# Small loads moved to GpSimd's DMA queue, stores issued later in the program, bias corners filled with the pair's scores

## The chip, the cores and the metric

The kernel runs on one core of a Trainium2 chip. The core has five engines that run side by side and wait for each other through semaphores: TensorE (PE in the profile, with PEld for its weight loads), VectorE (DVE), ScalarE (ACT), GpSimd (POOL) and SyncE (SP). A transfer between the chip's main memory and the on-chip memory is started by an instruction on the queue of one engine; here only SP starts any before the change. Each engine takes its instructions strictly in the order in which the program writes them. The metric is the device time of one execution in microseconds (us); lower is better.

## The reference

One inference step of a two-layer encoder on 320 tokens: 256 frames of a new stream ("prompt") and 64 next frames of an older one ("sample"). Cut to what matters:

```python
for l in range(2):
    h = x @ w_in[l]                                  # 1024 -> 3656 columns
    qa, ka, va, qb, kb, vb, qi, ki, wi = split(h)    # 8 heads of 64 each, twice; 8 index heads
    qb, kb, qi, ki = rope(qb), rope(kb), rope(qi), rope(ki)
    # A: 64-frame chunks read their own and earlier chunks, plus a learned bias of the distance
    oa = softmax(qa @ [cache_a_k, ka] / 8 + rel_bias[clip(distance)]) @ [cache_a_v, va]
    # B: an index score picks k keys for each query, attention over those
    score = sum_h wi[h] * relu(qi[h] @ [cache_b_kidx, ki])
    ob = softmax(over the top k of score)(qb @ [cache_b_k, kb] / 8) @ [cache_b_v, vb]
    x = layer_norm(alpha * x + concat(oa, ob) @ w_out[l])
    x = layer_norm(alpha * x + relu(x @ w_up[l])**2 @ w_down[l])
# returned: x, and ka, va, kb, vb, ki of both layers
```

## The kernel before

Activations are kept transposed (features on the 128 partitions, the 320 tokens along the free dimension), all in 32 bits. Every matrix product is done in three passes (`mm3`, L185 to L191): a weight block is split into a rounded high part `wh` and a rest `wl`, the activation likewise, and TensorE adds high x high, high x low and low x high (L188, L189, L190).

**Weights.** They come in units of 128 output columns (101 units in a layer). `load_raw` (L143) loads two units at a time, 1 MB, into one of two buffers `raw` (L151). `prefetch` (L160) has ScalarE write `wh` (L170), four units ahead of TensorE; a little later `split_rest` (L175) has VectorE write `wl` (L176), and when the second unit of a pair is split the `raw` buffer is free and the next load is written on SP. ScalarE's L170 waits for its load, and everything behind it on ScalarE waits too.

**Order of the work.** There is no scheduler: `manual_schedule` keeps each engine's instructions in the order in which the Python code writes them. A pretended clock (`clock`) moves on by `NEXT` (0.408 pretended us) with every `mm3`. `later(dt, fn)` (L118) puts a step on an agenda, and `advance` (L121) runs steps that are due between two `mm3`. `WAIT` (L46) holds the delays, by layer and by kind of step.

**Attention.** Heads go in pairs; `Pair` (L355) makes the tiles of one pair: queries, keys, values, and for kind A six loads of bias (`bias_tiles`, L333: for each of two heads a 128x128, a 128x256 and a 64x320 piece, L341) and two loads of cached keys and values (L367, L368). In a bias tile two 64x64 corners must hold a very negative number: GpSimd writes them (L342, L343) right behind the load. When a query tile is ready, GpSimd makes its "sample blocks" (`sample_blocks`, L346: one copy L351, two fills L352 and L353); the scores of the sample tokens (TensorE L396, or L535 for the index queries `qi`) wait for them. `scores` (L383), `peaks` (VectorE adds the bias, L410), `exps`, `normalise`, `turn` and `output` follow. The index (`Index`, L475) has four query tiles qi0 to qi3, taken in the order 0, 3, 2, 1; `dots` (L522) multiplies each with the keys (L533, L535).

**Stores.** New keys, values and index keys are stored by SP (L308, L317, L499, L771), written in the program at once behind the step that makes the tile, while that step still has to run on its engine.

All small tiles share 67 buffers named `u`.

Of the kernel before, what the change touches and what calls it, by code (L numbers as in the profile page):

```python
# [16 lines left out]
P = 128  # L17
# [16 lines left out]
NEG = -1.0e30  # L34
# [7 lines left out]
N_SIDE = 4  # L42
N_WARM = 7
N_TAIL = 4
TOKENS = slice(0, P), slice(P, 2 * P), slice(T - P, T)
WAIT = [{"lo": 3.4, "rope": 4.6, "scores": 3.4, "peaks": 0.0, "exps": 1.0, "normalise": 5.6, "turn": 3.0,  # L46
         "output": 2.0, "finish": 4.0, "value": 5.2, "keys": 6.0, "dots": 10.8, "clip": 0.0, "weigh": 0.2,
# [22 lines left out]
def encoder_step(ctx: ExitStack, tc: tile.TileContext, a: dict):  # L70
    nc = tc.nc
# [19 lines left out]
    def main_acc():  # L91
        return acc("mm", 8 - N_SIDE)
# [4 lines left out]
    def side_banks(n, fn, *args):  # L97

        if held[0] + n > N_SIDE:
            later(NEXT, fn, *args)  # L100
            return None
        held[0] += n
        return [acc("at", N_SIDE) for _ in range(n)]

    def release(n):
        held[0] -= n

    def unit(dt=F32, w=T):
        return st([P, 3 * P], "u", N_UNIT, dt)[:, :w]

    def temp(tag, bufs):
        return st([P, T], tag, bufs)
# [5 lines left out]
    def later(dt, fn, *args):  # L118
        agenda.append((clock[0] + dt, len(agenda), fn, args))

    def advance(dt):  # L121
        clock[0] += dt
        while agenda:
            i = min(range(len(agenda)), key=lambda i: agenda[i][0])
            if agenda[i][0] > clock[0]:
                break
            _, _, fn, args = agenda.pop(i)
            fn(*args)

    def flush():  # L130
        while agenda:
            advance(NEXT)
# [48 lines left out]
    def until(ready):  # L181
        while not ready():
            advance(NEXT)
# [97 lines left out]
    def evacuate(dst, src, scale=1.0):  # L281
        s, b = src
        if b is None:
            nc.scalar.activation(dst, s, AF.Copy, scale=scale)
        elif scale != 1.0:
            nc.vector.tensor_scalar(dst, s, b, scale, op0=ALU.add, op1=ALU.mult)
        else:
            nc.scalar.activation(dst, s, AF.Identity, bias=b, scale=scale)

    def swap(dst, src):  # L290
        for q in range(4):
            nc.scalar.activation(dst[32 * q:32 * q + 32], src[32 * (q ^ 1):32 * (q ^ 1) + 32], AF.Copy)  # L292

    def rotate(t, f, sw, c):
        nc.vector.tensor_tensor(t, f, rope[:, c], op=ALU.mult)
        nc.vector.tensor_tensor(sw, sw, rope[:, c + 1], op=ALU.mult)
        nc.vector.tensor_tensor(t, t, sw, op=ALU.add)

    def roped(t, src, c, out, then):

        f, sw = unit(), unit()
        evacuate(f, src)
        swap(sw, f)

        def turn():
            rotate(t, f, sw, c)
            if out is not None:
                nc.sync.dma_start(out, t)  # L308
            then()

        later(WAIT[l]["rope"], turn)

    def value(v, src, out, then):

        f = unit()
        evacuate(f, src)
        nc.sync.dma_start(out, f)  # L317

        def turn():
            got = side_banks(1, turn)  # L320
            if not got:
                return
            pt = got[0]
            release(1)
            for c, n in ((0, P), (1, P), (2, TS)):
                nc.tensor.transpose(pt[:n, c * P:(c + 1) * P], f[:, c * P:c * P + n], ident)
            nc.scalar.activation(v[:, 0:2], pt[:, 0:2 * P].rearrange("p (c d) -> p c d", c=2), AF.Copy)
            nc.scalar.activation(v[:TS, 2], pt[:TS, 2 * P:3 * P], AF.Copy)
            then()

        later(WAIT[l]["value"], turn)

    def bias_tiles(l, j):  # L333

        e = a["rel"]
        bp, bs = [unit(w=3 * P) for _ in range(2)], unit()
        for h in range(2):
            off = e.offset + (l * 8 + 2 * j + h) * N_DIST
            for dst, at0, n, m in ((bp[h][:, 0:P], 192, P, P), (bp[h][:, P:], 64, P, 2 * P),
                                   (bs[64 * h:64 * h + 64], 0, TS, NKEY)):  # L340
                nc.sync.dma_start(dst, bass.AP(tensor=e.tensor, offset=off + at0, ap=[[1, n], [1, m]]))  # L341
            nc.gpsimd.memset(bp[h][64:P, 64:P], NEG)  # L342
            nc.gpsimd.memset(bp[h][64:P, 5 * 64:6 * 64], NEG)  # L343
        return bp, bs

    def sample_blocks(f, at, keep):  # L346
# [8 lines left out]
    class Pair:  # L355


        def __init__(self, l, br, j, add):
            self.qf, self.k, self.v = unit(w=3 * P), unit(), unit(w=3 * P).rearrange("p (c d) -> p c d", c=3)
            self.o = unit(F32R), unit(F32R)  # L360
            self.flip = br == "a"
            self.q = self.qf[:, 64:] if self.flip else self.qf[:, :T]
            self.qs = self.qf[:, :P] if self.flip else self.qf[:, 2 * P:]
            nc.gpsimd.memset(self.v[TS:, 2], 0.0)
            self.add = add
            self.kc, self.vc = unit(w=PAST), unit(w=PAST).rearrange("p (c d) -> p c d", c=2)
            nc.sync.dma_start(self.kc, a["kc" + br][l, j])  # L367
            nc.sync.dma_start(self.vc, a["vc" + br][l, j])  # L368
            self.cols = (slice(192, T), slice(64, 192), slice(0, 64)) if self.flip else (
                slice(0, P), slice(P, 2 * P), slice(TP, T))  # L370
            self.have = set()
            self.done = False
# [10 lines left out]
        def scores(self):  # L383
            if not self.add:
                later(NEXT, self.scores)
                return
            q, k = self.q, self.k
            t0, t1, ts = self.cols
            banks = side_banks(3, self.scores)
            if not banks:  # L390
                return
            for t, c0, c1 in ((t0, 0, P), (t1, P, 3 * P)):
                for h, r in HALVES:
                    nc.tensor.matmul(banks[h][:, c0:c1], q[r, t], k[r, 0:c1 - c0], start=True, stop=True)  # L394
            for keys, c0, c1 in ((self.kc, 0, PAST), (k[:, TP:T], PAST, NKEY)):
                nc.tensor.matmul(banks[2][:, c0:c1], self.qs, keys, start=True, stop=True)  # L396
            later(WAIT[l]["peaks"], self.peaks, banks)

        def peaks(self, banks):
# [75 lines left out]
    class Index:  # L475


        def __init__(self, l):
            self.l = l
            self.qf = [unit(w=3 * P) for _ in range(4)]  # L480
            self.q = [q[:, :T] for q in self.qf]
            self.kx = unit(w=PAST)
            nc.sync.dma_start(self.kx, a["kidx"][l])
            self.mask = []
            self.k = self.w = None
            self.weighed = 0
# [9 lines left out]
        def turn(self):  # L496
            self.k = unit()
            rotate(self.k, self.kd, self.sw, 0)
            nc.sync.dma_start(a["o_ki"][self.l], self.k[0:64])  # L499
            self.weights()  # L500

        def weights(self):
# [160 lines left out]
    class LastNorm(Norm):  # L663
# [20 lines left out]
        def finish(self, psum):  # L684
            m, g, b, rg = KD - 1, self.g, self.b, self.rg
            r, sq = x[:, m], temp("sq", 2)
            on_pe = range(N_TAIL)
            pc, pm, pr = side_banks(3, None)
# [9 lines left out]
            def gather(c0, part, first=False, last=False):  # L698

                for i, t in enumerate(TOKENS):  # L700
                    nc.tensor.matmul(pc[:, c0 + i:c0 + i + 1], part[:, t], mean_w[:, 0:1], start=first and i == 0,
# [47 lines left out]
    for l in range(DEPTH):  # L749
# [4 lines left out]
        def take(name, j, src):  # L754
            if name == "ki":
                index.keys(src)
            elif name == "qi":
                roped(index.q[j], src, 0, None, lambda: index.got(j))
            else:
                p, kind, br = pairs[name[1], j], name[0], name[1]  # L760
                if kind == "v":
                    value(p.v, src, a["o_" + name][l, j], lambda: p.got("v"))
                elif br == "b":
                    roped(getattr(p, kind), src, 2 if kind == "q" else 0, a["o_kb"][l, j] if kind == "k" else None,
                          lambda: p.got(kind))
                elif kind == "q":
                    evacuate(p.q, (src[0][:, T - 1::-1], src[1]), scale=HD ** -0.5)
                    later(WAIT[l]["a"] - WAIT[l]["scores"] if kind == "k" else 0, p.got, kind)
                else:
                    evacuate(p.k, src)  # L770
                    nc.sync.dma_start(a["o_ka"][l, j], p.k)  # L771
                    later(WAIT[l]["a"] - WAIT[l]["scores"] if kind == "k" else 0, p.got, kind)

        uses = []
        for s, (name, j) in enumerate(W_IN_ORDER[l]):
            br = name[1]
# [18 lines left out]
        for m in range(KD):  # L795
            if m < N_OUTER:
                p = accs[m]
            else:
                prefetch(wo + m + AHEAD)
                p = main_acc()  # L800
# [26 lines left out]
        for m in range(KD):  # L827
            if m % 2 == 0:
                later(2.0, before.apply, m)
            p = main_acc()  # L830
# [102 lines left out]
```

## Time and profile before

| what | value |
|---|---|
| time of the runs | median 840.43 us of 3 (840.35 to 841.43) |
| the profiled execution, its own time | 836.99 us |
| its span, first to last instruction | 835.2 us |
| mean granted share of TensorE's clock | 0.993 |
| busy: PE, DVE, ACT, POOL | 98%, 71%, 59%, 3% of the span |
| q1, the queue that moves all of the kernel's data | 123.1 MB, 44.6% of 16 engines' span |

The profile is of one execution that took 836.99 us, 3.4 us less than the median of the runs. A busy TensorE is not a TensorE at its peak, since the records of matmuls overlap; what counts for it is when the next one starts, and at which granted clock. Layer 0's projection and attention lie at 4 to 165 us of the span, layer 1's at 416 to 568 us, the feed-forward parts between and behind them.

### The profile page before, as it was taken

The page shows a single profiled execution, that of the slowest core. Times are in us where ns is not written, and L with a number is a line of the kernel's source. Part 1 is how long each engine was busy: PE and PEld are TensorE (multiplying, and loading weights), DVE is VectorE, ACT ScalarE, POOL GpSimd, SP SyncE. Part 2 cuts the span into 40 slices and gives each one's busy share as a digit, 9 for nine tenths or more (in the row PEclk, how much of TensorE's full clock was granted, in tenths as well). Part 3 has the DMA queues.
Part 4 walks back from the last instruction along what each step waited for, and adds up shares of the span by engine and source line. Part 5 has one row for each costly group of instructions (what it writes and reads, how often), then busy time and mean ns, then how long its engine had stood idle before and what let it go on. Part 6 is the DMA issues. An engine that isn't in the chain of part 4 may idle for free.

```text
span 835.2 us, 15008 instructions
## 1 busy us (share of the span) xinstructions
PE 821.1 (98%) x5792; PEld 794.3 (95%) x5792; DVE 594.6 (71%) x1284; ACT 494.0 (59%) x955; POOL 28.7 (3%) x145
## 2 busy tenths in 40 slices
PE   9979999999999999999998999999999999999997
PEld 7969999999999999999998989999999999999995
DVE  5649878586998883545496679996699888545343
ACT  6846798565665553434358977885556655434332
POOL 0110000000000000000000010110000000000000
PEclk9999999999999999999999999999999999999998
DMA  8676343343444444534687324342334444434411
GB/s 275 192 191 180 135 143 126 125 151 103 151 156 147 152 154 149 177 127 155 194 171 261 108 101 135 120 177 74 136 145 151 152 151 152 160 144 152 151 51 64
DMA packets 35033, 124.05 MB, mean 149 GB/s; under 512 B 6033, under 2 KB 21521, under 8 KB 22290
## 3 DMA queue, kind: packets, MB, share of 16 engines
q1 hardware_dynamic: 34962, 123.10, 44.6%
q8 instruction: 46, 0.75, 0.4%
q14 instruction: 25, 0.20, 0.1%
HBM read 116.36 MB, written 6.72 MB: 147 GB/s over the span
## 4 chain that ended last, share of the span: by engine, by line
PE 75%; DVE 10%; ACT 8%; DMA 4%; SPq 1%; issue 1%; ACTq 0%; DVEq 0%
PE mm L188 23%; PE mm L189 23%; PE mm L190 23%; DMA raw<-w_all 4%; DVE wl L176 2%; ACT u L292 2%; ACT wh L170 2%; ACT u L418 1%; DVE u L577 1%; PE at L442 1%; DVE m L575 1%; PE at L394 1%; DVE u L410 1%; PE at L461 1%; PE at L396 1%
## 5 line engine op out<-in xcount | busy, mean ns | idle before, releaser
L188 PE MATMUL mm<-u,wh 128*128 128x320 f32 (+1 forms) x1048 | 328.8, 314 | 0.3 <-ACT wh L227 0.2
L190 PE MATMUL mm<-u,wl 128*128 128x320 f32 (+1 forms) x1048 | 324.0, 309 | 0.4 <-DVE wl L176 0.3
L189 PE MATMUL mm<-u,wh 128*128 128x320 f32 (+1 forms) x1048 | 323.8, 309 | 0.2 <-DVE u L233 0.2
L170 ACT ACTIVATE wh<-raw 128x1024 fp32r<-128x1024 f32 x199 | 209.5, 1055 | 182.9 <-PE mm L189 108.4
L176 DVE TENSOR_TENSOR wl<-raw,wh 128x1024 fp32r<-128x1024 f32 x199 | 241.3, 1217 | 57.8 <-ACT wh L170 57.3
L188 PEld LDWEIGHTS mm<-u,wh 128*128 128x128 f32 (+1 forms) x1048 | 196.8, 188 | 2.1 <-ACT wh L227 1.0
L190 PEld LDWEIGHTS mm<-u,wl 128*128 128x128 f32 (+1 forms) x1048 | 196.5, 187 | 1.6 <-DVE wl L228 0.9
L189 PEld LDWEIGHTS mm<-u,wh 128*128 128x128 f32 (+1 forms) x1048 | 196.9, 188 | 0.4 <-DVE u L233 0.4
L188 PE MATMUL mm<-rh,wh 128*128 128x322 f32 x568 | 177.5, 313 | 0.0
L190 PE MATMUL mm<-rh,wl 128*128 128x322 f32 x568 | 176.2, 310 | 0.0
L189 PE MATMUL mm<-rl,wh 128*128 128x322 f32 x568 | 175.8, 310 | 0.0
L189 PEld LDWEIGHTS mm<-rl,wh 128*128 128x128 f32 x568 | 107.2, 189 | 0.2
L188 PEld LDWEIGHTS mm<-rh,wh 128*128 128x128 f32 x568 | 107.1, 189 | 0.2
L190 PEld LDWEIGHTS mm<-rh,wl 128*128 128x128 f32 x568 | 106.5, 188 | 0.0
L603 DVE SCALAR_TENSOR_TENSOR x<-x,mm 128x320 f32<-128x320 f32 x31 | 15.0, 487 | 78.9 <-PE mm L190 78.9
L292 ACT ACTIVATE u<-u 32x320 f32<-32x320 f32 x104 | 48.7, 469 | 1.8
L270 DVE SCALAR_TENSOR_TENSOR z<-mu,mm 128x320 f32<-128x320 f32 x71 | 38.7, 545 | 12.7 <-PE mm L190 12.7
L811 ACT ACTIVATE z<-z,c 128x320 f32<-128x320 f32 x64 | 35.8, 560 | 16.8 <-DVE z L272 15.8
L418 ACT ACTIVATE u<-u,mx 128x128 f32<-128x128 f32 (+2 forms) x80 | 37.0, 464 | 8.9 <-DVE mx L413 8.9
L605 ACT ACTIVATE rh<-x,ln 128x320 fp32r<-128x320 f32 x24 | 13.5, 563 | 45.4 <-DVE x L603 45.4
L818 DVE TENSOR_TENSOR u<-h,u 128x320 fp32r<-128x320 f32 x64 | 31.5, 492 | 7.2 <-DVE h L817 0.5
L272 DVE TENSOR_TENSOR z<-z,rstd 128x320 f32<-128x320 f32 x71 | 34.9, 492 | 0.0
(135 smaller groups left out, 710.4 us busy)
## 6 DMA issues: line engine op xcount, KB each, us to landing
raw<-w_all SPq DMA_DIRECT2D x99, 1024.0 KB, 4.8
u<-rel SPq DMA_DIRECT2D x16, 128.0 KB, 5.5
u<-rel SPq DMA_DIRECT2D x16, 80.0 KB, 5.8
o_va<-u SPq DMA_DIRECT2D x8, 160.0 KB, 5.3
o_ka<-u SPq DMA_DIRECT2D x8, 160.0 KB, 2.3
o_kb<-u SPq DMA_DIRECT2D x8, 160.0 KB, 1.8
o_vb<-u SPq DMA_DIRECT2D x8, 160.0 KB, 1.8
o_y<-x SPq DMA_DIRECT2D x8, 160.0 KB, 1.9
```

The source lines that it names most:

```text
L170: nc.scalar.activation(hi, w, AF.Copy)
L176: nc.vector.tensor_tensor(lo, w, hi.bitcast(F32), op=ALU.subtract)
L188: nc.tensor.matmul(out, hi[:, k], xh, start=first, stop=False)
L189: nc.tensor.matmul(out, hi[:, k], xl, start=False, stop=False)
L190: nc.tensor.matmul(out, lo[:, k], xh, start=False, stop=last)
L270: nc.vector.scalar_tensor_tensor(u, mu[:n], p[:, T:T + 1], p[:, :T], op0=ALU.mult, op1=ALU.add)
L272: nc.vector.tensor_tensor(u, u, rstd[:n], op=ALU.mult)
L292: nc.scalar.activation(dst[32 * q:32 * q + 32], src[32 * (q ^ 1):32 * (q ^ 1) + 32], AF.Copy)
L418: nc.scalar.activation(p, p, AF.Exp, bias=self.mx[:, i:i + 1], scale=1.0, accum_out=self.sums[:, i:i + 1])
L603: nc.vector.scalar_tensor_tensor(r, r, ALPHA, psum, op0=ALU.mult, op1=ALU.add)
L811: nc.scalar.activation(u, u, AF.Relu, bias=b)
L818: nc.vector.tensor_tensor(hl, h, hh.bitcast(F32), op=ALU.subtract)
```

## The change

The six bias loads of each pair of kind A, the two cache loads of each pair of either kind, and the load of index keys in each layer, 82 in all, are written on GpSimd's queue and no longer on SP's. The four corner fills of a pair's bias tiles leave `bias_tiles` and are written in `scores`, behind the pair's score matmuls. Stores go through a new function `put`, which writes them on SP 10 pretended us later.

```diff
+STORE = 10.0
...
+    def put(out, t):
+
+        later(STORE, nc.sync.dma_start, out, t)
...
@@ roped, value, Index.turn and take: every store alike
-                nc.sync.dma_start(out, t)
+                put(out, t)
...
@@ bias_tiles
-                nc.sync.dma_start(dst, bass.AP(tensor=e.tensor, offset=off + at0, ap=[[1, n], [1, m]]))
-            nc.gpsimd.memset(bp[h][64:P, 64:P], NEG)
-            nc.gpsimd.memset(bp[h][64:P, 5 * 64:6 * 64], NEG)
+                nc.gpsimd.dma_start(dst, bass.AP(tensor=e.tensor, offset=off + at0, ap=[[1, n], [1, m]]))
...
@@ Pair.__init__
-            nc.sync.dma_start(self.kc, a["kc" + br][l, j])
-            nc.sync.dma_start(self.vc, a["vc" + br][l, j])
+            nc.gpsimd.dma_start(self.kc, a["kc" + br][l, j])
+            nc.gpsimd.dma_start(self.vc, a["vc" + br][l, j])
...
@@ Pair.scores, behind the score matmuls
+            if self.flip:
+                for b in self.add[0]:
+                    nc.gpsimd.memset(b[64:P, 64:P], NEG)
+                    nc.gpsimd.memset(b[64:P, 5 * 64:6 * 64], NEG)
             later(WAIT[l]["peaks"], self.peaks, banks)
...
@@ Index.__init__
-            nc.sync.dma_start(self.kx, a["kidx"][l])
+            nc.gpsimd.dma_start(self.kx, a["kidx"][l])
```

The order of the instructions on TensorE, VectorE and ScalarE stays as it was; SP has 154 rows for 236, GpSimd 232 for 150.

On SP, in layer 0, from the weight load of units 9 and 10 (`raw_299`) to that of units 11 and 12 (`raw_422`), the program writes before the change (`u_391` to `u_393` are the bias tiles of the first pair, `kca` and `vca` its cache):

```order
L151 DMA raw_299<-w_all 128x2048
L499 DMA o_ki<-u_325 64x320
L341 DMA u_391<-rel 128x128
L341 DMA u_391<-rel 128x256
L341 DMA u_393<-rel 64x320
L341 DMA u_392<-rel 128x128
L341 DMA u_392<-rel 128x256
L341 DMA u_393<-rel 64x320
L367 DMA u_410<-kca 128x256
L368 DMA u_411<-vca 128x256
L151 DMA raw_422<-w_all 128x2048
```

and after it, from the same load on (L156 is the weight load, L129 the delayed store; the second row is the load of units 11 and 12, the fourth that of units 13 and 14):

```order
L156 DMA raw_299<-w_all 128x2048
L156 DMA raw_417<-w_all 128x2048
L129 DMA o_ki<-u_325 64x320
L156 DMA raw_556<-w_all 128x2048
L156 DMA raw_659<-w_all 128x2048
L156 DMA raw_806<-w_all 128x2048
L129 DMA o_va<-u_599 128x320
L129 DMA o_ka<-u_400 128x320
```

The loads between the weight loads are gone from SP, and the stores stand further down; between the loads of units 11 and 12 and of units 13 and 14 stood sixteen small loads before, and one store stands there now.

On GpSimd, in layer 0, at the second pair's bias corners and the sample blocks of the first pair's queries (`u_404`) and of qi1 (`u_170`), before:

```order
L342 MEMSET u_452 64x64
L343 MEMSET u_452 64x64
L342 MEMSET u_453 64x64
L343 MEMSET u_453 64x64
L364 MEMSET u_467 64x128
L351 COPY u_404<-u_404 64x64
L352 MEMSET u_404 64x64
L353 MEMSET u_404 64x64
L351 COPY u_170<-u_170 64x64
L352 MEMSET u_170 64x64
L353 MEMSET u_170 64x64
```

and the same place after (`u_399` are the first pair's queries, `u_449` a bias tile of the second pair; five more bias loads of that pair stand right ahead of these rows, and eight loads of the first pair ahead of qi2's blocks before them):

```order
L346 DMA u_449<-rel 64x320
L367 MEMSET u_458 64x128
L370 DMA u_462<-kca 128x256
L371 DMA u_463<-vca 128x256
L354 COPY u_399<-u_399 64x64
L355 MEMSET u_399 64x64
L356 MEMSET u_399 64x64
L354 COPY u_170<-u_170 64x64
L355 MEMSET u_170 64x64
L356 MEMSET u_170 64x64
```

The corner fills, which waited for their loads, have left this place; in their stead sixteen loads in all are issued by GpSimd between the blocks of qi3 and those of qi1. In layer 1 the loads of all four A pairs, thirty-two, stand in one row ahead of the first pair's blocks.

## Rows read from the trace of the kernel before

**Rows 1.** The page's first part: busy time, share of the span, instructions

```profile
PE 821.1 (98%) x5792; PEld 794.3 (95%) x5792; DVE 594.6 (71%) x1284; ACT 494.0 (59%) x955; POOL 28.7 (3%) x145
```

**Rows 2.** Waits of PE over the span: total us, times, longest

```profile
PE at L394 <- ACT u L328: 2.6, 1, 2.6
PE at L394 <- ACT u L288: 2.4, 1, 2.4
PE at L533 <- ACT u L541: 1.7, 1, 1.7
```

**Rows 3.** Four windows: length, busy us of each engine (instructions), clock, DMA share, GB/s

```profile
5.00:10.00 5.00, 4.48 (x23) 2.99 (x23) 3.10 (x8) 3.24 (x9) 0.00 (x0) 1.00 1.00 309
24.82:31.82 7.00, 7.00 (x50) 7.00 (x49) 5.46 (x11) 6.82 (x13) 0.64 (x3) 1.00 0.43 154
59.00:65.78 6.78, 6.78 (x25) 5.95 (x26) 6.46 (x25) 4.67 (x9) 0.00 (x0) 0.50 0.19 67
60.00:70.00 10.00, 10.00 (x52) 9.16 (x50) 9.96 (x39) 6.96 (x20) 0.15 (x1) 0.71 0.47 82
```

**Rows 4.** Timeline of ACT: start, us, what [idle before, what ended it]

```profile
43.98 1.06 ACT L170 ACTIVATE wh<-raw 128x1024 fp32r<-128x1024 f32 x1 [4.97 <-DMA raw<-w_all]
...
57.42 1.06 ACT L170 ACTIVATE wh<-raw 128x1024 fp32r<-128x1024 f32 x1 [8.61 <-DMA raw<-w_all]
...
446.48 1.06 ACT L170 ACTIVATE wh<-raw 128x1024 fp32r<-128x1024 f32 x1 [3.38 <-DMA raw<-w_all]
```

**Rows 5.** Timeline of SP's queue, layer 0 and the start of layer 1

```profile
35.95 0.37 SPq L151 DMA_DIRECT2D raw<-w_all  x1
36.59 4.91 SPq L341 DMA_DIRECT2D u<-rel  x6
...
48.53 0.36 SPq L151 DMA_DIRECT2D raw<-w_all  x1
...
409.24 3.45 SPq L341 DMA_DIRECT2D u<-rel  x6
...
439.18 0.38 SPq L151 DMA_DIRECT2D raw<-w_all  x1
```

**Rows 6.** Timeline of DVE: the splits that free a weight buffer

```profile
33.00 1.23 DVE L176 TENSOR_TENSOR wl<-raw,wh 128x1024 fp32r<-128x1024 f32 x1 [0.23 <-ACT wh L170]
...
40.30 1.21 DVE L176 TENSOR_TENSOR wl<-raw,wh 128x1024 fp32r<-128x1024 f32 x1
...
436.75 1.22 DVE L176 TENSOR_TENSOR wl<-raw,wh 128x1024 fp32r<-128x1024 f32 x1
```

**Rows 7.** DMA issues of the page: KB each, median us from issue to landing

```profile
raw<-w_all SPq DMA_DIRECT2D x99, 1024.0 KB, 4.8
```

**Rows 8.** Timeline of POOL: sample blocks and a fill

```profile
32.83 0.23 POOL L351 COPY u<-u 64x64 f32<-64x64 f32 x1 [3.10 <-DVE u L297]
...
33.31 0.14 POOL L353 MEMSET u<- 64x64 f32 x1
...
45.34 0.20 POOL L364 MEMSET u<- 64x128 f32 x1
...
46.34 0.47 POOL L351 COPY u<-u 64x64 f32<-64x64 f32 x1
```

**Rows 9.** Timeline of PE: sample scores of qi1, first pairs' scores in layers 0 and 1

```profile
51.87 0.87 PE L535 MATMUL at<-u,u 128*128 128x256 f32 x4
...
58.96 2.02 PE L394 MATMUL at<-u,u 64*128 64x128 f32 x8 [2.65 <-ACT u L328]
...
450.28 0.87 PE L396 MATMUL at<-u,u 128*128 128x256 f32 x4
```

**Rows 10.** The bias tensor's issues on SP: duration ns min/median/max, first and last start

```profile
L341 SPq DMA_DIRECT2D u<-rel x48: 328/472/833, 30.9 to 437.0; - x48
```

**Rows 11.** Timeline of DVE and of POOL at one moment of layer 1

```profile
539.53 1.22 DVE L176 TENSOR_TENSOR wl<-raw,wh 128x1024 fp32r<-128x1024 f32 x1
539.75 1.10 POOL L351 COPY u<-u 64x64 f32<-64x64 f32 x1 [9.96 <-DVE u L297]
```

More of the change, by code (lines that the diff above doesn't have):

```diff
@@ L316, in value @@
         evacuate(f, src)
-        nc.sync.dma_start(out, f)
+        put(out, f)
         def turn():
@@ L498, in turn @@
             rotate(self.k, self.kd, self.sw, 0)
-            nc.sync.dma_start(a["o_ki"][self.l], self.k[0:64])
+            put(a["o_ki"][self.l], self.k[0:64])
             self.weights()
@@ L770, in take @@
                     evacuate(p.k, src)
-                    nc.sync.dma_start(a["o_ka"][l, j], p.k)
+                    put(a["o_ka"][l, j], p.k)
                     later(WAIT[l]["a"] - WAIT[l]["scores"] if kind == "k" else 0, p.got, kind)
```

## The prediction

> **What bounds the kernel now.** I read the engines' totals first: PE is busy 98% of the span, nothing else over 71% [rows 1]. So only a moment in which PE waits, or runs slower, can be given back. The second view is therefore PE's own waits, and they are few [rows 2]: 2.6 us for ScalarE's L328, 2.4 us for its L288, 1.7 us for its L541. Third, the windows, for the clock [rows 3]: at 24.82 to 31.82 us PE starts 50 matmuls in 7.00 us at clock 1.00; at 59.00 to 65.78 us it starts 25 in 6.78 us at clock 0.50, which is 1.2 instead of 2.4 GHz. That slow stretch begins right behind the 2.6 us wait, and it costs half its length, 6.78 x 0.5 = 3.4 us. Behind the 2.4 us wait of layer 1 I saw no such stretch. All that PE loses in these places is 1.7 + 2.6 + 3.4 + 2.4 = 10.1 us of 835.2.
>
> Fourth, why ScalarE is late at these three places: its timeline shows it each time at L170, held for a weight load, 4.97, 8.61 and 3.38 us long, until 43.98, 57.42 and 446.48 us [rows 4]. What PE needs stands behind that L170 on ScalarE. Fifth, why the load is late: SP's timeline has the three loads issued at 35.95, 48.53 and 439.18 us [rows 5], while the splits that free their buffers end at 33.00 + 1.23 = 34.23, 40.30 + 1.21 = 41.51 and 436.75 + 1.22 = 437.97 us [rows 6]. SP was busy with small loads in between: six bias issues alone took it 4.91 us from 36.59 on [rows 5]. And the loads are slow: they land 43.98 - 35.95 = 8.0, 57.42 - 48.53 = 8.9 and 446.48 - 439.18 = 7.3 us after issue, where the median of such a load is 4.8 us [rows 4, 5, 7], because small loads stand ahead of them in the same queue.
>
> **What the change takes away.** SP now holds only weight loads and delayed stores at these places, so a weight load goes out when its buffer is free.
>
> Load 2 (units 13, 14) can go out at 41.51 instead of 48.53 us. Landing takes 4.8 us if undisturbed and 8.9 us if it is disturbed as before, so it lands between 46.3 and 50.4 us. PE came to its 2.6 us wait at 58.96 - 2.65 = 56.3 us [rows 9]. Even the late end leaves ScalarE over 5 us for what it owes PE. I take off the whole 2.6 us and the 3.4 us of half clock: 6.0.
>
> Load 1 (units 11, 12) goes out at 34.23 and lands at 39.0 to 42.3 us, against 43.98 before. It moves PE's release by 1.7 us or more at either end (43.98 - 42.3 = 1.7): 1.7 off.
>
> Load 3 (layer 1) goes out at 437.97, lands at 442.8 to 445.3 us. At the late end it is 1.2 us earlier than 446.48, at the early end all of the 2.4 us goes. I take 2.0, since no more than one pair's loads should be left beside it.
>
> **What it adds.** GpSimd issues 82 loads, in the same order of program as its sample blocks, and PE waits for those blocks. No row shows a load issued by GpSimd. Below, its price is bounded by the same loads' issues on SP, 0.47 us in the median [rows 10]; nothing lower is likely, as the queue only changes its issuer. Above, I use that issue plus one hold by VectorE: a GpSimd copy that takes 0.23 us when free [rows 8] took 1.10 us beside a split on VectorE, and ended with it (539.53 + 1.22 = 540.75, 539.75 + 1.10 = 540.85) [rows 11]. That makes 0.47 + 1.10 = 1.57 us. Between ends so far apart I take the middle, 1.0 us, as neither is nearer.
>
> The Trainium skill ("DMA: Bandwidth & Descriptors", Specifications) gives about 1 us until the first byte of a transfer from GpSimd's queue against 0.6 us from SP's; as a price per issue that would be the same 1.0 us, and no row here shows it.
>
> In layer 0 the first place where this bites is the sample scores of qi1. GpSimd ends qi3's blocks at 33.31 + 0.14 = 33.45 us, a set of blocks takes 33.45 - 32.83 = 0.62 us, a fill 0.20 [rows 8]. Ahead of qi1's finished blocks now stand 16 loads, two fills and three sets of blocks: 33.45 + 0.40 + 1.86 + 16 x price = 35.7 + 16 x price. Before, GpSimd began that copy at 46.34 us [rows 8]. PE reached L535 for qi1 at 51.87 us, and will at 51.87 - 1.7 = 50.1 us without its earlier wait [rows 9, 2]. No wait arises up to a price of 0.90; at 1.0 it is 51.7 - 50.1 = 1.6 us; at 0.47 none, at 1.57 10.7 us. Queued behind the loads are also the first pair's corner fills, 24 loads down, and VectorE's L410 behind those.
>
> In layer 1, 32 loads stand ahead of the first pair's blocks. If GpSimd starts when SP did, at 409.24 us [rows 5], the blocks are done at 409.24 + 0.8 (four fills) + 0.62 + 32 x price = 442.7 us at 1.0. PE wants them at 450.28 - 2.4 = 447.9 us [rows 9, 2]; no wait up to a price of 1.16, 13 us at 1.57.
>
> The index keys' 128 KB now start with the first loads of all instead of behind them. There the transfer engines are full, at 309 GB/s and share 1.00 [rows 3]: 128 KB / 309 GB/s = 0.4 us, added to the start. The bounds are 0 and 0.4.
>
> The stores' later place costs nothing that I can find: SP has the time, and what they held up were weight loads. It would cost only if a reused buffer waits for a store that itself stands behind a weight load. The corner fills cost GpSimd the same as before, hidden under its idle time.
>
> Finally, PE's pauses were cover for VectorE, which is busy 9.96 of 10 us at 60 to 70 us [rows 3]. With PE some 7 us earlier there, part of that comes back as waits for VectorE. I put 1.5 us, an estimate between 0 and the 4.3 us of PE's two pauses that gave VectorE time.
>
> **The sum**, on the profiled execution: 835.2 - 6.0 - 1.7 - 2.0 + 1.6 + 0.4 + 1.5 = 829.0 us of span, 6.2 less. Its own time was 836.99, and the median of the runs 840.43 lies 3.4 above that; 840.4 - 6.2 = 834.2 us. A measurement of this kernel can tell about 0.2%, 1.7 us, from no change.
>
> **Rivals.** First, the issue is cheap (under 0.90 us) and VectorE keeps up: no added waits but the start, 840.4 - 9.7 + 0.4 = 831 us. For it speaks that SP's issues take half a microsecond; against it that GpSimd's work was stretched by VectorE in [rows 11].
>
> Second, no gain: the small loads now run beside a weight load instead of ahead of it, on the same transfer engines, and the load that goes out at 41.51 still lands near 57 us. Then only the pause moves from one place to another, plus 0.4 at the start: about 841 us. Against it: the load that landed in 8.9 us had sixteen small ones ahead of it, and it now starts 7.0 us earlier.
>
> The Trainium skill ("DMA: Bandwidth & Descriptors", Issuing engines are not separate DMA queues) says just this, that transfers started on several engines share the same 16 transfer engines, and that only the issuer's time is saved. By that rule this second rival holds as far as the engines were full, and the trace agrees in part: SP's issue time was a good share of the delay, 7.0 us of it at load 2.
>
> Third, slower: GpSimd's issues are dear. Above 1.18 us a load, PE's wait at qi1 (4.5 us and more) brings the half clock back, and the gain of layer 0 is spent; at 1.3 us the wait is 35.7 + 20.8 - 50.1 = 6.4 us in place of 1.7 + 2.6, so layer 0 loses 2.1 with the half clock as before, layer 1 waits (1.30 - 1.16) x 32 = 4.5 instead of 2.4, and with the 1.9 of the other terms the time is 840.4 + 2.1 + 2.1 + 1.9 = 846.5 us; at 1.57 it is near 860. For it speaks the held copy [rows 11] and that VectorE has work for nearly all of 60 to 70 us [rows 3]; against it that the copy reads on-chip memory and an issue need not.
>
> The Trainium skill ("SBUF — State Buffer", SBUF: two separate sides) warns of this very change: GpSimd can't write a transfer's descriptors while VectorE runs certain instructions that take the port both share, and a queue of SP is free of that. By that rule the third rival's price holds wherever VectorE runs such instructions; the held copy is the only sign of it in this trace.
>
> **Chances.** Forecast (price 0.9 to 1.1, VectorE's share anywhere in its bounds, 832 to 838 us) 0.43; cheap issue (about 831) 0.15; no gain, by the second rival or by a price near 1.18 (839 to 842), 0.14; dear issue (842 and up) 0.28. Faster by over 0.2%: 0.58; within 0.2%: 0.14; slower: 0.28. The range goes from 829.5, all of the waits gone, to 846, a price of 1.3; it leaves out the dearer half of the third rival and little else. The forecast's own range is 832 to 838.
>
> **What would show it.** In the changed kernel's profile: weight loads issued near 34, 41.5 and 438 us and ScalarE's three long waits at L170 gone or under 2 us; PE's waits for L328 and L541 gone, the clock at 1.00 around 59 to 66 us; GpSimd issues of about 1 us each, and PE's longest new wait at qi1's L535 (L542 by the new numbering), for GpSimd. If those issues take 1.3 us or more, or if PE waits 5 us there or at layer 1's first sample scores, the forecast is wrong by its price; if the loads go out early and still land at 57 us, it is wrong by the second rival.

## The result and the profile after

The changed kernel takes 831.13 us in the median of 4 runs (830.27 to 833.54), the kernel before 840.39 us beside it (838.57 to 841.43): a ratio of 0.9897, with an interval of 0.9870 to 0.9924. Timed a second time on another chip it was 831.26 against 838.67 us, 0.9913 (0.9892 to 0.9935). The profiled execution of the changed kernel has a span of 829.1 us, 6.1 less than that of before; its own time is 830.85 us. So the gain is 0.9 to 1.0% by the runs and 0.7% by the two traces.

The engines' totals of the changed kernel (busy us, share of the span, instructions), to be read beside [rows 1]:

```profile
PE 817.8 (99%) x5792; PEld 791.5 (95%) x5792; DVE 594.7 (72%) x1284; ACT 493.8 (60%) x955; POOL 71.9 (9%) x227
```

GpSimd has 82 instructions more, the loads, and 43 us more of work. PE has lost only idle time and half-clock time. Its waits after the change (total us, times, longest), beside [rows 2]:

```profile
PE at L540 <- ACT u L453: 1.5, 1, 1.5
PE at L540 <- ACT u L548: 1.4, 2, 0.8
PE mm L193 <- DVE c L276: 1.2, 1, 1.2
PE mm L228 <- POOL mean_w L206: 1.0, 1, 1.0
PE mm L193 <- ACT wh L232: 0.8, 1, 0.8
PE mm L195 <- DVE wl L181: 0.7, 1, 0.7
```

The waits of 2.6 and 2.4 us at the first pairs' scores (L394 before, L397 now) are gone. L548 is the clip that was L541. No wait for GpSimd's sample blocks is there. The clock between 59.00 and 65.78 us, beside the third of [rows 3] (same columns), and the last stretch of the span:

```profile
59.00:65.78 6.78, 6.78 (x52) 6.49 (x50) 6.75 (x25) 5.06 (x15) 2.72 (x9) 1.00 0.81 218
823.49:831.10 7.61, 1.75 (x3) 0.50 (x2) 0.98 (x3) 1.97 (x5) 0.00 (x0) 0.50 0.45 155
```

PE starts 52 matmuls where it started 25, at clock 1.00. The only half clock left is the last stretch, which the kernel before has too; its window reaches past the last instruction at 829.1 us.

Next SP's queue of the changed kernel, beside [rows 5]. The three weight loads go out at 35.25, 42.64 and 433.35 us, with nothing but delayed stores behind them (the load of 433.35 is the one of 439.18 before: the first behind the load of w_ki, which itself went out at 431.60 us before):

```profile
35.25 0.33 SPq L156 DMA_DIRECT2D raw<-w_all  x1
35.62 1.31 SPq L129 DMA_DIRECT2D o_ki<-u  x1
42.64 0.34 SPq L156 DMA_DIRECT2D raw<-w_all  x1
...
425.14 0.65 SPq L152 DMA_DIRECT2D raw<-w_ki  x1
433.35 0.34 SPq L156 DMA_DIRECT2D raw<-w_all  x1
```

ScalarE's timeline, beside [rows 4], tells when they land:

```profile
43.82 1.06 ACT L175 ACTIVATE wh<-raw 128x1024 fp32r<-128x1024 f32 x1 [3.82 <-DMA raw<-w_all]
...
48.82 1.06 ACT L175 ACTIVATE wh<-raw 128x1024 fp32r<-128x1024 f32 x1 [0.16 <-DMA raw<-w_all]
...
438.50 1.06 ACT L175 ACTIVATE wh<-raw 128x1024 fp32r<-128x1024 f32 x1 [1.19 <-DMA raw<-w_all]
```

Load 2 lands 8.6 us earlier than before (57.42 to 48.82), load 3 8.0 us (446.48 to 438.50). Of these 8.0 us the place itself has won only 3.3: PE comes to layer 1's first scores 4.7 us earlier in any case, for what layer 0 gained (the last matmul ahead of them starts at 442.06 us, before at 446.72). Load 1 lands when it always did, though SP issued it 0.7 us sooner. Last, GpSimd's timeline between qi3's blocks and qi1's, beside [rows 8]:

```profile
34.32 0.15 POOL L356 MEMSET u<- 64x64 f32 x1
34.41 3.20 POOL L346 DMA_DIRECT2D u<-rel  x6
...
39.49 0.54 POOL L346 DMA_DIRECT2D u<-rel  x1
41.34 0.54 POOL L346 DMA_DIRECT2D u<-rel  x1 [1.31 <-DMA u<-rel]
43.83 2.15 POOL L346 DMA_DIRECT2D u<-rel  x4 [1.95 <-DMA u<-rel]
...
47.30 1.14 POOL L354 COPY u<-u 64x64 f32<-64x64 f32 x1
...
49.37 0.14 POOL L356 MEMSET u<- 64x64 f32 x1
```

Six loads take 3.20 us, 0.53 each, and twice GpSimd waits for an earlier load to land before it issues the next; none of the first nine loads of the row waits, the tenth and the eleventh do. qi1's blocks are done at 49.37 + 0.14 = 49.51 us; PE starts the scores that need them at 51.72, so 2.2 us were to spare.

### The profile page after: what moved, and what is told of

It is laid out like the page before. It is cut to its first block, busy times and chain, and to the rows that moved or that the text cites. A ratio compares the mean times of both kernels' runs of the same rounds, so it can differ in the third digit from the quotient of the medians.

```text
span 829.1 us, 15032 instructions
## 1 busy us (share of the span) xinstructions
PE 817.8 (99%) x5792; PEld 791.5 (95%) x5792; DVE 594.7 (72%) x1284; ACT 493.8 (60%) x955; POOL 71.9 (9%) x227
## 4 chain that ended last, share of the span: by engine, by line
PE 78%; DVE 5%; ACT 2%; DMA 1%; issue 0%; ACTq 0%
PE mm L193 24%; PE mm L194 24%; PE mm L195 23%; PE at L449 1%; DVE wl L181 1%; PE at L468 1%; DVE u L584 1%; DMA raw<-w_all 1%; DVE m L582 1%; PE at L397 1%; PE at L399 1%; PE at L471 1%; PE at L331 0%; PE at L540 0%; PE mm L703 0%
## 5 line engine op out<-in xcount | busy, mean ns | idle before, releaser
L181 DVE TENSOR_TENSOR wl<-raw,wh 128x1024 fp32r<-128x1024 f32 x199 | 241.6, 1218 | 59.8 <-ACT wh L175 59.5
L346 POOL DMA_DIRECT2D u<-rel x48 | 25.8, 541 | 229.0 <-DVE x L610 213.6
```

The costliest lines, as they stand in the source:

```text
L181: nc.vector.tensor_tensor(lo, w, hi.bitcast(F32), op=ALU.subtract)
L346: nc.gpsimd.dma_start(dst, bass.AP(tensor=e.tensor, offset=off + at0, ap=[[1, n], [1, m]]))
```

## The experiments

Each kernel ran beside the kernel before, and the ratios are to that. Where two of them are compared, they ran on the same chip, but for the changed kernel itself, which was timed beside the last versions only; against the others it is set by the ratios and the traces.

**The stores alone.** The kernel before, with this:

```diff
-                nc.sync.dma_start(out, t)
+                put(out, t)
```

and the same at the three other places of the change.

> The kernel before with the stores alone issued later; small loads stay on SP. Theory A (SP's own time for the small loads is what held up the weight loads, and stores cost nothing there): 840.4 us as before, within 1.7; the weight loads are still issued near 36 and 48.5 us and ScalarE's hold until 57.4 us and PE's 2.6 us wait stay. Theory B (stores that wait on SP for their producers hold the weight loads behind them): 836 us or less, and the load of 48.5 us goes out earlier.

Measured: 835.23 us against 837.73, 0.9975 (0.9960 to 0.9990). Neither theory is whole. PE's waits:

```profile
PE at L399 <- ACT u L333: 2.8, 1, 2.8
PE at L538 <- ACT u L451: 1.1, 1, 1.1
...
PE at L538 <- ACT u L546: 0.2, 1, 0.2
```

The wait at the first pair's scores in layer 0 and the half clock behind it are as before (the load issued at 47.19 us held ScalarE until 56.07; the clock is 0.50 from 57.02 to 63.85 us), so small loads cause those. But two waits are gone. One is layer 0's wait for the clip, 1.74 us before and 0.2 here: load 1 goes out at 34.96 us and is there by 41.59, with the small loads still on SP. In the trace of before the store of the index keys, at 30.25 us, stood ahead of the first pair's loads, which began at 30.86 us; here they begin at 28.62.

```profile
41.59 1.06 ACT L175 ACTIVATE wh<-raw 128x1024 fp32r<-128x1024 f32 x1 [1.88 <-DMA raw<-w_all]
```

The other is the wait of layer 1: there it was enough that the stores left. In the trace of before, a store of o_va stands ahead of each of two sets of eight small loads there, at 426.63 and 432.32 us, a third at 438.71, and w_ki and the weight load behind them:

```profile
426.63 0.34 SPq L317 DMA_DIRECT2D o_va<-u  x1
427.07 3.33 SPq L341 DMA_DIRECT2D u<-rel  x6
430.50 0.53 SPq L367 DMA_DIRECT2D u<-kca  x1
431.13 0.38 SPq L368 DMA_DIRECT2D u<-vca  x1
431.60 0.61 SPq L147 DMA_DIRECT2D raw<-w_ki  x1
```

With the stores later, w_ki goes out at 428.14 us instead of 431.60, and the weight load at 436.35 instead of 439.18. PE is 1.6 us ahead here (445.07 us for the 446.72 above), so 1.8 and 1.2 us of this are won at the place itself.

**The loads without the later stores.** The changed kernel, with this:

```diff
-        later(STORE, nc.sync.dma_start, out, t)
+        nc.sync.dma_start(out, t)
```

> The changed kernel with its stores issued at once again, all else as changed. Theory A: 831 us, within 1.7, as SP without the small loads has time for the stores. Theory B (a store that waits for its producer holds the weight load behind it on SP): 835 us or more, with a weight load issued later than 42.6 us and ScalarE held for it.

Measured: 829.98 us against 837.73, 0.9925 (0.9899 to 0.9952). Theory A holds: once the small loads are off SP, the stores' place is worth nothing that these runs can tell. Its trace has weight loads at 35.14 and 42.50 us and neither of the two long waits.

**One layer at a time.** The changed kernel, with this in all four places (and with l == 1 in a second kernel):

```diff
-            nc.gpsimd.dma_start(self.kc, a["kc" + br][l, j])
+            (nc.gpsimd if l == 0 else nc.sync).dma_start(self.kc, a["kc" + br][l, j])
```

> The changed kernel with layer 1's small loads back on SP. The traces put 4.7 us of the gain ahead of layer 1 and 2.5 us at the first sample of layer 1, where PE's 2.4 us wait for ScalarE is gone; the medians differ by 3 us more than the two traces do. Theory A (that remainder is a second stretch of half clock, behind the wait of layer 1, which most executions of the kernel before have and its traced one has not): the wait of layer 1 is back and the time is 840.4 - 4.7 = 835.7 us, up to 837. Theory B (the remainder lies in layer 0): 831.1 + 2.5 = 833.6 us or less.

> The changed kernel with layer 0's small loads back on SP. Theory A (a second stretch of half clock belongs to layer 1's wait): 840.4 - 2.5 - 3.4 = 834.5 us, PE's 2.6 us wait near 56 to 59 us and the half clock behind it as before, none in layer 1. Theory B (layer 1 is worth only the 2.5 us of its wait, the rest lies in layer 0): 840.4 - 2.5 = 837.9 us.

Measured: layer 0 alone 830.58 us, 0.9930 (0.9904 to 0.9956); layer 1 alone 836.43 us, 0.9996 (0.9975 to 1.0017). My theory of a second stretch of half clock behind layer 1's wait falls: with layer 1's small loads on SP nothing is lost that the runs can tell, and that wait is not back. The weight load of layer 1 goes out at 430.96 us, w_ki ahead of it at 422.76, with PE 7.0 us ahead (439.68 us for 446.72):

```profile
422.76 0.61 SPq L152 DMA_DIRECT2D raw<-w_ki  x1
423.46 3.63 SPq L346 DMA_DIRECT2D u<-rel  x6
...
430.96 0.33 SPq L156 DMA_DIRECT2D raw<-w_all  x1
```

So in layer 1 either part of the change removes the wait, and the loads' move to GpSimd earns its gain in layer 0; what it costs in layer 1 is told below, under VectorE. Layer 1 alone keeps layer 0's wait (3.4 us at L397) with its half clock, and its median is not below that of the stores alone.

**The price of an issue.** The changed kernel, with this ahead of every bias and cache load (and with six fills in a second kernel):

```diff
+    idle = ct([P, P], "idle")
+    def slow():
+        for _ in range(3):
+            nc.gpsimd.memset(idle, 0.0)
...
+                slow()
                 nc.gpsimd.dma_start(dst, ...)
```

> The changed kernel with three fills of a spare 128x128 tile on GpSimd ahead of each bias and cache load: an issue costs about 0.54 + 3 x 0.15 = 1.0 us, the price that the prediction took. By the prediction's formula PE then waits 35.7 + 16 x 1.0 - 50.1 = 1.6 us at qi1's sample scores, nothing in layer 1: 831.1 + 1.6 = 832.7 us. Rival (GpSimd's queue keeps its waits for landings and only adds the fills to the 49.5 us at which qi1's blocks were done): blocks at 49.5 + 16 x 0.46 = 56.9 us, PE, which came there at 51.7, waits 5.2 us, with a stretch of half clock behind it: 831.1 + 5.2 + 3.4 = 839.7 us.

> The same with six fills ahead of each load: an issue costs about 1.4 us, inside the prediction's third rival. By its formula PE waits 35.7 + 16 x 1.4 - 50.1 = 8.0 us at qi1, with half clock behind it, and (1.4 - 1.16) x 32 = 7.7 us in layer 1: 831.1 + 8.0 + 3.4 + 7.7 = 850 us, slower than before. Rival (layer 1's GpSimd starts early enough or the wait there is hidden): only the first wait, 842 to 844 us.

Measured: 846.62 us, 1.0087 (1.0058 to 1.0116), and 891.37 us, 1.0618 (1.0589 to 1.0646). The fills are dearer than I had put them. GpSimd's timeline with three fills:

```profile
34.42 0.53 POOL L353 DMA_DIRECT2D u<-rel  x1
34.95 0.75 POOL L342 MEMSET idle<- 128x128 f32 x3
35.65 0.54 POOL L353 DMA_DIRECT2D u<-rel  x1
```

A step takes 1.23 us here and 1.31 later on (loads at 45.65 and 46.96 us), 1.27 in the middle, so this kernel stands where my third rival stood (1.3). At that price the prediction's formula gives 35.7 + 16 x 1.27 - 50.1 = 5.9 us of waiting; the expectation's rival, which keeps the landing waits, gives 49.5 + 16 x 0.73 - 51.7 = 9.5. PE's timeline:

```profile
57.11 1.54 PE L551 MATMUL at<-u,u 128*128 128x256 f32 x4 [6.48 <-POOL u L363]
```

The formula is right to 0.6 us, and GpSimd's waits for landings are gone in this trace, hidden by the slower issues. Of the layer-1 wait, (1.27 - 1.16) x 32 = 3.5 us by the formula, nothing came: PE ran 7.0 us later than before, but GpSimd began these loads at 410.21 us, only 1.0 later than the formula's 409.24. Earlier, until 83.84 us, PE waits 3.1 us for ScalarE's L289. With six fills a step takes 2.0 us (loads at 36.02 and 38.02 us). The formula gives 35.7 + 16 x 2.0 - 50.1 = 17.6 us ahead of qi1's scores and (2.0 - 1.16) x 32 = 27 us in layer 1; the waits:

```profile
PE at L408 <- POOL u L363: 21.9, 1, 21.9
PE at L551 <- POOL u L363: 17.6, 2, 10.9
```

The 17.6 us come in two parts (qi2's scores and qi1's), layer 1's wait is there with 21.9. That the first agrees to the tenth is luck, since PE ran at clock 0.50 for part of the time between the two waits. The clock is down for long here, from 482.68 to 506.57 us among others, which the formula doesn't have; so the time is 891 us where the expectation, at a lower price, had 850.

**The corner fills.** The changed kernel, with the fills back behind the loads:

```diff
+            nc.gpsimd.memset(bp[h][64:P, 64:P], NEG)
+            nc.gpsimd.memset(bp[h][64:P, 5 * 64:6 * 64], NEG)
...
-            if self.flip:
-                for b in self.add[0]:
-                    nc.gpsimd.memset(b[64:P, 64:P], NEG)
-                    nc.gpsimd.memset(b[64:P, 5 * 64:6 * 64], NEG)
```

> The changed kernel with the corner fills back behind the loads that they overwrite. Theory A (a fill waits on GpSimd until its load has landed, and the next loads and the sample blocks stand behind it): two landings of about 6 us for each pair, so qi1's blocks come some 10 us or more later than 49.5 us, PE waits over 5 us at its sample scores with half clock behind it, and the time is 840 us or more. Theory B (GpSimd waits for earlier loads anyway, so the fills cost nothing): 831 us, within 2.

Measured: 863.12 us, 1.0297 (1.0256 to 1.0339). Theory A holds, and more than at the one place that I named: PE waits for sample blocks three times, 19.4 us in all. GpSimd's own waits:

```profile
POOL u L347 <- DMA u<-rel: 50.7, 16, 4.7
...
POOL u L348 <- DMA u<-rel: 22.7, 16, 2.5
```

All 32 fills hold the queue, 73.4 us in all. The loads' move is a gain only together with the fills' move: apart from it, it makes the kernel 3% slower.

**The index keys.** The changed kernel, with this:

```diff
-            nc.gpsimd.dma_start(self.kx, a["kidx"][l])
+            nc.sync.dma_start(self.kx, a["kidx"][l])
```

> The changed kernel with the index keys' load back on SP's queue, behind the first loads. Theory A (their 128 KB at the start compete with the first loads): PE's second unit starts 0.4 to 0.5 us earlier and the time is about 0.5 us less, 830.6, which these rounds can hardly tell from 831.1; the trace decides. Theory B: the start is unchanged.

Measured: 830.41 us, 0.9894 (0.9863 to 0.9925), which can't be told from the changed kernel. Nor does the trace settle it: PE's early waits for L232 and L181 add to 1.5 us in the changed kernel, to 1.0 in its second trace and to 0.5 here, but to 1.6 in another kernel that has the index keys on SP (the layer-0 version below).

**Why load 1 stays slow.** The changed kernel, with this ahead of the first pair's loads:

```diff
+        if (l, j) == (0, 0):
+            for _ in range(40):
+                nc.gpsimd.memset(idle, 0.0)
```

> The changed kernel with 40 spare fills on GpSimd (about 0.24 us each) ahead of the first pair's loads in layer 0, so that they start near 44 us instead of 34.4. It is for one reading: when the weight load issued near 35.3 us lands, 43.8 us in the changed kernel. Theory A (it shares full transfer engines with those loads): alone it lands in about 4.9 us, the median of such loads, so near 40.2 us, and ScalarE's 3.8 us hold shrinks to under 1 us. Theory B (something else makes that load slow): it lands near 43.8 us as before. The time itself is no evidence: the blocks of qi1 come about 10 us later, PE waits for them some 7 us, and the run takes 843 us or more.

Measured: one run, 836.77 us (PE's wait for qi1's blocks is 5.0 us). The reading that it was made for, on ScalarE's timeline:

```profile
40.41 1.06 ACT L175 ACTIVATE wh<-raw 128x1024 fp32r<-128x1024 f32 x1 [0.42 <-DVE u L567]
```

Issued at 35.23 us, the load is there by 40.41, at most 5.2 us later, and ScalarE's last wait is not for it. Theory A holds, by one trace. In the changed kernel the engines that carry the loads were full meanwhile; the window from its issue to its landing there (columns as in [rows 3]):

```profile
35.25:43.80 8.55, 7.71 (x52) 6.94 (x51) 6.46 (x13) 4.70 (x10) 5.18 (x13) 1.00 0.95 241
```

**Versions that might be better.** Two combinations, beside the changed kernel itself: index keys on SP with stores at once, and layer 1's loads and all index keys on SP with stores later. Their edits are those shown above.

> The changed kernel itself, timed again beside the two versions below and the kernel before: ratio 0.989 to 0.993, where all runs of it and its near variants have lain. Its traced execution has no half clock but a last stretch; where that stretch is longer than 7.6 us, the span is longer by half of the difference.

> The changed kernel with the index keys' load back on SP and the stores issued at once: of the change's three parts only the bias and cache loads on GpSimd and the later fills are left. Theory A (these two alone give the gain, the index keys cost 0.5 us at the start): 830.5 us on the same chip as the changed kernel's 831, 0 to 1 us less. Theory B (the later stores give a part): 1 to 3 us more than the changed kernel.

> The changed kernel with layer 1's small loads and both loads of index keys on SP, stores issued later. Theory A (in layer 1 the later stores alone free SP enough for the weight loads, as in the run with layer 1's loads on SP): as the changed kernel or up to 1 us less; no wait of PE for ScalarE's sample copy in layer 1. Theory B: 2 us or more above the changed kernel.

Measured: 831.26 us (830.98 to 832.46), 0.9913 (0.9892 to 0.9935), for the changed kernel, as expected; 829.22 us (829.02 to 830.89), 0.9893 (0.9868 to 0.9918), for the first combination; 830.68 us (828.62 to 834.15), 0.9911 (0.9887 to 0.9935), for the second. The first is 2.0 us less than the changed kernel in the medians; their runs just don't overlap, their intervals do. That is Theory A's side, by more than it said. It has the lowest median, by little, and with the run above it shows no part of the gain that needs the later stores once the loads have moved. The second has no wait for the sample copy in layer 1, as its Theory A said.

## Why the prediction was right, and where it was off

The forecast was 834.2 us with a range from 829.5 to 846.0, and faster as the likeliest sign. The time lies inside the range, at the figure of the first rival, the cheap issue (about 831), which I had given 0.15. By span the sum said 829.0, and the trace has 829.1; but that is partly luck, as four of its terms were off and made up for each other. The forecast was 3.1 us too long for another reason, the 3.4 us that I added to get from the trace to the median: the traced execution of the changed kernel, 830.85 us, stands at its median. And the first rival's figure is met by luck too. Its price was right, but it let PE wait for nothing but the start, which takes 9.3 us off the span; the spans differ by 6.1. (The low end of my range, 829.5, called "all of the waits gone", is not what my figures give for that, 840.4 - 10.1 = 830.3.)

Where the 6.1 us come from can be read at matmuls that both traces have: PE is 6.1 us ahead where the half clock of before ends (59.46 for 65.56), 4.7 on the way to layer 1's first scores (442.06 for 446.72), 7.1 at them (442.30 for 449.42), and 6.3 at the last norm (819.50 for 825.77).

**The wait of layer 0 and its half clock: 6.0, right.** The wait of 2.65 us and the stretch at 0.50 are both gone, and the run with the stores alone, which keeps both, and that with the loads alone, which has neither, show that the small loads on SP were their cause. Load 2 left SP at 42.64 us (I had 41.51) and landed in 6.2, inside my 4.8 to 8.9.

**Load 1: 1.7 forecast, about 0.3 measured.** The step "goes out at 34.23 and lands at 39.0 to 42.3" failed. It went out at 35.25, as the split that frees its buffer ended a microsecond later, and landed at 43.8. PE's wait for the clip shrank from 1.74 us to 0.6, but 0.84 us appeared at the one before; ScalarE's hold, which was to be under 2 us, is 3.82. The second rival, no gain because the transfers share their engines, is true of this load: the DMA share is 0.95, and the held pair shows that the load takes 5.2 us at most when the small loads are away. The Trainium skill ("DMA: Bandwidth & Descriptors", Issuing engines are not separate DMA queues) says so, and here the trace agrees. At load 2 it does not stand in the way, because SP's hold had been the larger part. With the stores alone moved, this load landed by 41.59 us: here it was the store that stood in the way, and the small loads' move spent what the stores' move had won.

**Layer 1: 2.0 forecast, 2.4 gone.** The step held, the reason was half of it. The load went out at 433.35 us and ScalarE had it at 438.50; with PE's lead of 4.7 us added, that is 438.0 and 443.2 in the time of before, where I had 437.97 and 442.8 to 445.3. But I had put the load's lateness down to the small loads and wrote that the stores' later place "costs nothing", without a gain for it. Either move alone removes this wait. Of the gain some goes back at once: PE's next wait for ScalarE, 0.63 us before, is 1.47.

**The price of an issue: 1.0 forecast, 0.54 measured.** This is the step that was mis-sized. Between 0.47 and 1.57 I took the middle, and the lower end was the right neighbour: the same loads, issued by another engine, take the same kind of time. All issues of the bias tensor on GpSimd (duration ns min/median/max):

```profile
L346 POOL DMA_DIRECT2D u<-rel x48: 532/538/566, 34.4 to 421.5; - x48
```

No issue was stretched, though VectorE was busy for 6.75 of 6.78 us at 59 us, where some of them fell; a copy of GpSimd beside it still was (1.14 us at 47.30). The rule of the Trainium skill ("SBUF — State Buffer", SBUF: two separate sides), that VectorE can keep GpSimd from writing descriptors while it runs certain instructions, I looked for as long issues; no issue in this trace shows it. Whether VectorE ran such instructions beside them no run here tells. The added wait at qi1, 1.6 us, therefore never came.

What I had not seen is that a queue waits for earlier loads to land: of GpSimd's 49.51 us at qi1, 1.31 + 1.95 = 3.3 us are such waits. SP had them before the change, 3.6 us between 36 and 48.6 us, so its hold of load 2, which I read as issue time, was in part such waits; the eighth of its sixteen small loads waited for load 1 itself to land (SP's own waits over the span, total us, times, longest):

```profile
SPq L368 <- DMA raw<-w_all: 2.5, 2, 1.8
...
SPq L341 <- DMA u<-rel: 2.5, 4, 1.0
```

With 35.7 + 16 x 0.54 = 44.3 for the formula, 1.0 for a start that came later (34.47 instead of 33.45), 3.3 for the waits and 0.9 for the held copy it is 49.5, and the kernel at 1.27 us confirms the formula itself in layer 0. That kernel takes 846.62 us, where the third rival had 846.5 at 1.3, which is luck as well: it lacks that rival's wait in layer 1 and has others (3.1 us at L289). In layer 1 the formula's start was wrong: GpSimd doesn't begin when SP did, at 409.24 us, but as soon as buffers are free, with four loads from 182.80 us on and the next at 398.50.

**The start: 0.4 forecast, not settled.** The traces differ there by as much whichever queue carries the index keys.

**VectorE gives back: 1.5 forecast, not seen.** PE has a new wait of 1.24 us, for VectorE's L276 behind the reciprocal of the first norm. But VectorE was not short of time there: it stood idle ahead of that reciprocal, for ScalarE, and ScalarE had been held by a weight load (GpSimd, SP, ScalarE, VectorE and PE of the changed kernel):

```profile
182.80 0.54 POOL L490 DMA_DIRECT2D u<-kidx  x1 [42.92 <-PE mm L194]
183.33 1.59 POOL L346 DMA_DIRECT2D u<-rel  x3
184.62 0.33 SPq L156 DMA_DIRECT2D raw<-w_all  x1
193.08 1.06 ACT L175 ACTIVATE wh<-raw 128x1024 fp32r<-128x1024 f32 x1 [2.56 <-DMA raw<-w_all]
196.70 2.15 DVE L645 RECIPROCAL rstd<-rstd 128x320 f32<-128x320 f32 x1 [1.71 <-ACT rstd L644]
199.44 0.39 PE L193 MATMUL mm<-rh,wh 128*128 128x322 f32 x1 [1.24 <-DVE c L276]
```

GpSimd, with nothing else to do by then, issues layer 1's index keys and its first three bias loads some 220 us before SP did. The weight load that SP issues beside them takes 8.4 us, and the DMA share is 0.88 until it lands. In the kernel with layer 0's loads alone on GpSimd the same load, issued at 183.69 us, is there before ScalarE turns to it at 188.54 (share 0.61), and PE doesn't wait. Over all fourteen traces, the four with layer 1's loads on SP have no such wait; of the ten with them on GpSimd nine have it, 0.5 to 1.2 us, and the tenth is the kernel with six fills, where these loads go out at another moment. So this is the second rival once more, at a place where I had looked for nothing. PE comes to the last norm at 819.50 and 819.47 us in the two traces of the changed kernel, and at 816.84 and 817.02 in those of the two versions with layer 1's loads on SP. Part of that lead is lost again in their longer last stretch, and the medians don't show it.

**The corner fills' later place** I had costed at nothing and called hidden. That is right for the new place, but I didn't say what it averts: 863.12 - 831 = 32 us.

**Timed and traced.** The medians differ by 9.3 and 7.4 us, the spans by 6.1. The 30 runs of before beside the first eight experiments lie between 835.45 and 841.23 us, so its traced execution at 836.99 is one of the quicker ones, and the 3.4 us that I added for this are scatter of that kernel. I first took them for a second stretch of half clock behind layer 1's wait; the layer-0 kernel refuted that place. But the scatter does go with the clock: of these 30 runs the eight with a mean granted clock of 0.995 have spans of 833.4 to 834.9 us, the three with 0.985 or 0.987 of 838.8 to 839.4. In which stretch the clock was down, runs without a trace don't tell; that stays open.

## What to carry to other kernels

Where large loads leave late, count all that their engine issues ahead of them, the stores that wait for their producers too, and ask of each moved load two things apart: when it can go out, and whether the transfer engines have room for it then. An engine with little else to do issues its loads as soon as buffers are free, here some 220 us early and beside a weight load that PE needed. Before loads move to an engine that also computes, look for what on that engine must wait for a landing: here the corner fills behind their own loads turn a gain of 1% into a loss of 3%. And price an issue by the same transfer's issue elsewhere; then work out from which price on the next consumer waits, since in layer 0 that formula outlived a wrong price.

## What the runs showed that I had not expected

Kernels that end with the same instructions run at half clock there for very different lengths. In the changed kernel the last stretch holds 1.75 us of busy PE (the window shown above). In the trace of the kernel with layer 1's loads alone on GpSimd, whose span is 837.5 us, the last window reads:

```profile
822.84:839.80 16.96, 10.44 (x17) 3.95 (x15) 5.90 (x14) 5.30 (x13) 0.00 (x0) 0.50 0.23 79
```

There 17 matmuls of the last norm run at 0.50, and half of 10.44 us is 5.2 us lost. What sets the length no run here shows. That kernel's twelve runs go from 833.32 to 842.09 us. A comparison to 1% of such a kernel needs many executions, and one trace can mislead by some microseconds at the end alone.
